# Softmax over 16384 rows: first loads issued from two queues, and a short store of zeros dropped

## The chip, the cores and the metric

The kernel runs on one core of a Trainium2 chip. The metric is device time in microseconds (us), from the start to the end of one execution; the median of several executions is used. A profile of one execution gives the span between its first and last recorded instruction, and a trace of all instructions and DMA transfers in it.

## The reference

The input x has the shape (32, 512, 1024) in float32 and the temperature is 0.5. The last axis is softmaxed:

```
scaled = x / temperature
shifted = scaled - max(scaled, axis=-1)
exp_x = exp(shifted)
out = exp_x / sum(exp_x, axis=-1)
```

That is 16384 rows of 1024 numbers: 67.1 MB are read and 67.1 MB are written.

## The kernel before

The rows are cut into 16 tiles of 1024 rows. A tile holds 8 rows in each of the 128 partitions, that is 32 KB in a partition and 4 MB (4096 KB) in all. There are six buffers for tiles (`BUFS = 6`, pool `data`). A tile is read into its buffer by one DMA, worked on in place, and written from the same buffer by one DMA.

The work on a tile comes in two groups of four rows per partition. For each group there are four steps:

- `maximum` (L70, L73): VectorE (DVE) takes the maximum of four rows in one TENSOR_REDUCE and multiplies it by -1/temperature, which gives a bias.
- `exponential` (L79): ScalarE (ACT) computes exp(x / temperature + bias) for one row per partition at a time, four times, and sums each row on the way.
- `divide` (L91, L93): DVE takes the reciprocal of the sums and multiplies the four rows by it.
- `store` (L101): after the second group of a tile, ACT's queue issues the store of the whole tile. Then `load` is called for the tile six places further on; this load goes to the buffer just stored, and so waits until the store has landed.

The order is written out by hand in the last loop: maximum and exponential of group g stand before divide and store of group g-1, so DVE takes the maximum of group g while ACT may still be at group g-1, and divides group g-1 while ACT works on group g.

All loads (L61) are issued from SP's queue, in the order of the tiles; all stores are issued from ACT's. An instruction that issues a DMA stands in the order of its engine: it waits for its semaphores there, and what is behind it on that engine waits too. SP does nothing but issue loads.

Ahead of the loop stand three things. DVE fills a small tile, `zeros`, of 512 bytes per partition (L111). ACT's queue issues a store of it into the first 128 columns of one row per partition of the first output tile (L112); the proper store of that tile later overwrites it. Then the first six loads are called.

Of the kernel before, what the change touches and what calls it, by code (L numbers as in the profile page):

```python
# [1 line left out]

# [4 lines left out]

TILES = [[8]] * 16  # L10
BUFS = 6

GROUP = 4


@with_exitstack
def kernel(
    ctx: ExitStack,
    tc: tile.TileContext,
    x: bass.AP,  # L20
    temperature: bass.AP,
    out: bass.AP,
):
    nc = tc.nc
    f32 = mybir.dt.float32
    scale = 1.0 / float(temperature)
    extreme = mybir.AluOpType.max if scale > 0 else mybir.AluOpType.min

    P = 128
    xf = x.flatten_outer_dims()  # L30
    of = out.flatten_outer_dims()
    n, d = xf.shape
    assert sum(sum(ks) for ks in TILES) * P == n

    data = ctx.enter_context(tc.tile_pool(name="data", bufs=BUFS))
    stats = ctx.enter_context(tc.tile_pool(name="stats", bufs=4))


    groups, first, r = [], [], 0
    for i, ks in enumerate(TILES):  # L40
        first.append(r)
        r += sum(ks)
        a = 0
        for k in ks:
            for b in range(0, k, GROUP):
                m = min(GROUP, k - b)
                groups.append((i, a + b, m, (a, k) if b + m == k else None))
            a += k

    def dram(t, i):  # L50
        k = sum(TILES[i])
        block = t[P * first[i] : P * (first[i] + k), :]
        return block.rearrange("(p k) d -> p k d", p=P, k=k)

    tiles, small = [], []

    def load():
        i = len(tiles)
        if i < len(TILES):
            xt = data.tile([P, sum(TILES[i]), d], f32, name="xt")  # L60
            nc.sync.dma_start(out=xt, in_=dram(xf, i))  # L61
            tiles.append(xt)

    def maximum(g):
        i, a, k, _ = groups[g]
        top, bias, sums, recip = (
            stats.tile([P, k], f32, name=name) for name in ("top", "bias", "sums", "recip")
        )
        small.append((bias, sums, recip))
        nc.vector.tensor_reduce(  # L70
            out=top, in_=tiles[i][:, a : a + k, :], axis=mybir.AxisListType.X, op=extreme
        )
        nc.vector.tensor_scalar_mul(bias, in0=top, scalar1=-scale)  # L73

    def exponential(g):
        i, a, k, _ = groups[g]
        bias, sums, _ = small[g]
        for b in range(k):
            nc.scalar.activation(  # L79
                tiles[i][:, a + b, :],  # L80
                tiles[i][:, a + b, :],
                mybir.ActivationFunctionType.Exp,
                bias=bias[:, b : b + 1],
                scale=scale,
                accum_out=sums[:, b : b + 1],
            )

    def divide(g):
        i, a, k, _ = groups[g]
        _, sums, recip = small[g]  # L90
        nc.vector.reciprocal(recip, sums)  # L91
        for b in range(k):
            nc.vector.tensor_scalar_mul(  # L93
                tiles[i][:, a + b, :], in0=tiles[i][:, a + b, :], scalar1=recip[:, b : b + 1]
            )

    def store(g):
        i, _, _, part = groups[g]
        if part:
            a, k = part  # L100
            nc.scalar.dma_start(out=dram(of, i)[:, a : a + k, :], in_=tiles[i][:, a : a + k, :])  # L101
            if a + k == sum(TILES[i]):
                load()

    zeros = stats.tile([P, 128], f32, name="zeros", bufs=1)
    with tc.manual_schedule():


        nc.vector.memset(zeros, 0.0)  # L111
        nc.scalar.dma_start(out=dram(of, 0)[:, 0, :128], in_=zeros)  # L112
        for _ in range(BUFS):
            load()
        for g in range(len(groups) + 1):
            if g < len(groups):
                maximum(g)
                exponential(g)
            if g > 0:
                divide(g - 1)  # L120
                store(g - 1)


# [1 line left out]
_INS = ['x', 'temperature']  # L125
_OUTS = [((32, 512, 1024), 'float32')]

_NUMBERS = {'temperature': 0.5}


# [26 lines left out]
```

## Time and profile before

| | |
|---|---|
| median of 4 runs | 318.34 us (318.18 to 318.73) |
| time of the profiled execution | 318.18 us |
| its span | 316.4 us |
| DVE busy | 235.6 us (74%) |
| ACT busy | 149.6 us (47%) |
| HBM read and written | 67.11 MB and 67.17 MB, 424 GB/s over the span |
| DMA packets | 4756, of which 528 under 512 bytes and 656 under 2 KB |
| a load, median time from issue to landing | 49.4 us |
| a store, the same | 39.4 us |
| the store of zeros, the same | 14.6 us |

The profile names a group of instructions by its line in the code, its engine, and the tile that it writes and reads: `xt<-in_x_dram` is a load, `out_dram<-xt` a store. SPq and ACTq are the queues from which DMAs are issued. The busy share of an engine is an average over the whole span; in the row of 40 slices each digit is the busy share in one fortieth (7.9 us), in tenths, and 9 stands for 90% or more. The time from issue to landing of a DMA holds the time that it stood behind others in its queue.

### The profile page before, as it was taken

How to read it: one execution, taken by the hardware profiler on the slowest of the kernel's cores; microseconds unless marked ns; L12 is line 12 of the kernel's file. 1: busy time of each engine (PE TensorE's matmuls, PEld its weight loads, DVE VectorE, ACT ScalarE, POOL GpSimd, SP SyncE). 2: the span in 40 equal slices, each digit the busy share in tenths (PEclk: the TensorE clock that was granted, in tenths of full speed). 3: DMA queues.
4: the chain of work that ended last, by engine and by line, in shares of the span. 5: the costliest groups of instructions: out<-in, count | busy, mean ns of one | idle time of the engine just before them, and what ended most of it. 6: DMA issues, size and time to landing. Idle time of an engine off the chain costs nothing.

```text
span 316.4 us, 623 instructions
## 1 busy us (share of the span) xinstructions
DVE 235.6 (74%) x225; ACT 149.6 (47%) x257; POOL 0.2 (0%) x4
## 2 busy tenths in 40 slices
DVE  0399999999689494994949859497793976949720
ACT  0176666666526255361554606556164561645500
POOL 0000000000000000000000000000000000000000
DMA  8999999999999999999999999999999999999995
GB/s 333 404 464 414 377 460 406 460 429 427 443 418 456 406 456 410 452 410 460 406 456 427 435 432 431 447 414 452 414 452 407 456 406 460 410 456 423 439 431 244
DMA packets 4756, 134.32 MB, mean 425 GB/s; under 512 B 528, under 2 KB 656, under 8 KB 656
## 3 DMA queue, kind: packets, MB, share of 16 engines
q1 hardware_dynamic: 2304, 67.11, 49.6%
q10 hardware_dynamic: 2448, 67.18, 49.2%
q14 instruction: 4, 0.03, 0.0%
HBM read 67.11 MB, written 67.17 MB: 424 GB/s over the span
## 4 chain that ended last, share of the span: by engine, by line
DMA 61%; DVE 28%; ACT 4%; another core or an unknown queue 1%; issue 1%; DVEq 0%; SPq 0%
DMA xt<-in_x_dram 35%; DMA out_dram<-xt 25%; DVE top L70 18%; DVE xt L93 9%; ACT xt L79 4%; DVE bias L73 1%; DVE recip L91 0%; DVEq L152 0%; SPq L61 0%
## 5 line engine op out<-in xcount | busy, mean ns | idle before, releaser
L79 ACT ACTIVATE xt<-xt,bias 128x1024 f32<-128x1024 f32 x128 | 145.4, 1137 | 136.8 <-DVE recip L91 119.4
L70 DVE TENSOR_REDUCE top<-xt 128x4 f32<-128x4096 f32 x32 | 141.3, 4416 | 61.7 <-DMA xt<-in_x_dram 61.7
L93 DVE TENSOR_SCALAR xt<-xt,recip 128x1024 f32<-128x1024 f32 x128 | 87.7, 749 | 1.1
L79 ACT ACTIVATION_READ_ACCUMULATOR xt<-xt,bias 128x1 f32 x128 | 23.8, 186 | 0.0
L79 ACT ACT_TABLE_LOAD x1 | 1.3, 1283 | 13.2 <-DMA xt<-in_x_dram 13.2
L91 DVE RECIPROCAL recip<-sums 128x4 f32<-128x4 f32 x32 | 5.5, 171 | 2.1 <-ACT xt L79 2.1
L73 DVE TENSOR_SCALAR bias<-top 128x4 f32<-128x4 f32 x32 | 5.4, 170 | 1.1
L111 DVE MEMSET zeros<- 128x128 f32 x1 | 0.2, 165 | 0.8 <-PEq L138 0.8
L138 POOL MEMSET const-uint8-127<- 128x1 uint8 x1 | 0.1, 103 | 0.0
L138 POOL MEMSET const-bfloat16-1.0<- 128x1 bf16 x1 | 0.1, 102 | 0.0
L138 POOL MEMSET const-float32-0.0<- 128x1 f32 x1 | 0.1, 99 | 0.2 <-issue 0.2
L138 POOL MEMSET const-float32-1.0<- 128x1 f32 x1 | 0.1, 99 | 0.0
## 6 DMA issues: line engine op xcount, KB each, us to landing
xt<-in_x_dram SPq DMA_DIRECT2D x16, 4096.0 KB, 49.4
out_dram<-xt ACTq DMA_DIRECT2D x16, 4096.0 KB, 39.4
out_dram<-zeros ACTq DMA_DIRECT2D x1, 64.0 KB, 14.6
```

What stands on the lines that cost most here:

```text
L70: nc.vector.tensor_reduce(out=top, in_=tiles[i][:, a : a + k, :], axis=mybir.AxisListType.X, op=extreme)
L73: nc.vector.tensor_scalar_mul(bias, in0=top, scalar1=-scale)
L79: nc.scalar.activation(tiles[i][:, a + b, :], tiles[i][:, a + b, :], mybir.ActivationFunctionType.Exp, bias=bias[:, b : b + 1], scale=scal ...
L91: nc.vector.reciprocal(recip, sums)
L93: nc.vector.tensor_scalar_mul(tiles[i][:, a + b, :], in0=tiles[i][:, a + b, :], scalar1=recip[:, b : b + 1])
L111: nc.vector.memset(zeros, 0.0)
L138: nc = _bacc.Bacc("TRN2", target_bir_lowering=False, num_devices=1)
```

## The change

The second, fourth and sixth of the six loads that first fill the buffers are issued from ACT's queue; the first, third and fifth, and all later loads, are issued from SP's as before. The tile `zeros`, its memset and its store are gone.

```diff
         if i < len(TILES):
             xt = data.tile([P, sum(TILES[i]), d], f32, name="xt")
-            nc.sync.dma_start(out=xt, in_=dram(xf, i))
+
+            queue = nc.scalar if i < BUFS and i % 2 else nc.sync
+            queue.dma_start(out=xt, in_=dram(xf, i))
             tiles.append(xt)
...
-    zeros = stats.tile([P, 128], f32, name="zeros", bufs=1)
     with tc.manual_schedule():
-
-
-        nc.vector.memset(zeros, 0.0)
-        nc.scalar.dma_start(out=dram(of, 0)[:, 0, :128], in_=zeros)
         for _ in range(BUFS):
             load()
```

On ACT the three loads now stand ahead of everything else: the load of the table for exp, the exponentials and the stores.

## The prediction
> **What bounds the kernel now.** I read the slices of the span first, then the table by stretches, then the waits, and last the chain.
>
> ```profile
> DVE  0399999999689494994949859497793976949720
> ACT  0176666666526255361554606556164561645500
> DMA  8999999999999999999999999999999999999995
> ```
>
> The DMA engines are full from the first slice to the last. DVE and ACT are full only until about 85 us; after that they wait. So the time is bytes over rate, plus whatever the DMA engines lose. The stretches below give that rate (the columns are the stretch, its length, busy DVE, ACT and POOL, clock, DMA share, GB/s).
>
> ```profile
> 5.00:31.00 26.00, 17.51 (x14) 11.46 (x18) 0.00 (x0) 1.00 1.01 435
> 31.00:41.00 10.00, 9.93 (x11) 7.25 (x15) 0.00 (x0) 1.00 0.99 393
> 41.00:90.00 49.00, 44.84 (x43) 28.84 (x50) 0.00 (x0) 1.00 1.00 432
> 90.00:280.00 190.00, 145.55 (x140) 92.58 (x160) 0.00 (x0) 1.00 1.00 433
> 283.00:312.00 29.00, 17.40 (x19) 9.28 (x16) 0.00 (x0) 1.00 1.00 432
> ```
>
> 5 to 31 us holds loads (and the small store of zeros); 41 to 280 loads and stores together; 283 to 312 stores alone. All run at 432 to 435 GB/s, so it makes no difference which kind is moved. The exception is 31 to 41 us, where the first large store (issued at 32.84) joins the running loads: 393 instead of 433 over 10 us, a loss of 10 x 40 / 433 = **0.92 us**. I call it the turn. The rest follows: 134.3 MB at 433 GB/s is 310.2 us, the turn 0.9, and 5.3 us of span are the start (first load issued at 0.73) and the thin end. The profiled execution took 318.18 us, 1.8 us more than its span of 316.4.
>
> ```profile
> DVE top L70 <- DMA xt<-in_x_dram: 61.7, 12, 12.2
> ...
> SPq L61 <- DMA out_dram<-xt: 215.8, 10, 44.6
> SPq L61 <- DMA xt<-in_x_dram: 9.9, 1, 9.9
> ```
>
> DVE waits 12 times for a load, SP's queue 10 times for a store that frees a buffer. SP waits once for a load: its sixth load was held until the first had landed at 13.1 us. None of these waits leaves the DMA engines idle, because another transfer is always queued. At the end:
>
> ```profile
> 232.93 49.80 DMA xt<-in_x_dram
> ...
> 282.75 4.43 DVE top L70
> ...
> 301.16 1.32 DVE xt L93 x2
> ```
>
> The last load lands at 282.7, and its store is issued at 302.5. The store before it, issued at 290.26, takes 15.4 us to land (305.7), so the DMA engines have work until 3.2 us after the last store is issued. The last store lands 12.8 us after its issue, at 315.3.
>
> **The change, part by part.**
>
> *Zeros removed.* One memset of 0.17 us on DVE, at 0.83, where DVE then waits 12.15 us for the first load: free. One issue of 0.41 us on ACT at 1.02, where ACT idles until 13.2: free. The first large store no longer follows it to the same output rows, but the zeros landed at 1.02 + 14.6 = 15.6, long before 32.84: free. What counts is 65.5 KB on the bound resource: 0.0655 MB / 433 GB/s = **-0.15 us**.
>
> *Three loads moved to ACT's queue.* By the order of instructions, ACT now issues three loads ahead of its table load and first exponential, and SP three, then ten. An issue took 0.36 to 0.56 us at this place on SP, so three are at most 1.7 us on ACT, under at least 12 us of idle time: free. The first packets can't come earlier, since SP's first load is first in its queue in both kernels.
>
> *The first tile lands later.* Loads 0 and 1 now run side by side. Before, load 0 landed at 13.1 and load 1 at 22.8 (issued at 1.1, 21.7 to landing). Shared evenly, both land at about 22: the bounds are 13.1, if SP's is served first, and 22.8. I take 22, nearest to even sharing. That two queues share evenly I take from the same table of issues: a load spaced 9.7 us from the next alone, a store every 19.35 us (134.49 to 153.84) when a load runs beside it. DVE starts 9 us later, and store 0 is issued at 22 + 19.7 = 42 instead of 32.84 (the first tile took 13.14 to 32.84). The cover is that the DMA engines keep loading: the loads come in pairs at 22, 42 and 61. DVE needs 14.8 us a tile (stores at 32.84, 47.61, 62.39), 237 us in all, and from 22 it could end at 264 with the last store's lag: well before the end.
>
> *Stores wait behind loads.* Stores 0 (42) and 1 (57) are queued behind load 5 on ACT's queue and start at about 61, alone, because all six buffers are full and SP has nothing to issue. Store 0 lands at about 71; then SP issues load 6. At 61 there is work for 2 x 9.7 us, to 80 us; store 2 comes at 72 and load 6 at 71, so the engines don't run dry. Without that cover, each us of idle time would cost a us. Load 6 lands at 91 to 95, before DVE asks for it at 22 + 6 x 14.8 = 111. From then on loads and stores alternate as before. ACT itself waits only for DVE at each store, as now.
>
> *The end.* Loads have the engines to themselves until 61 instead of about 35 (half of 26 us gained for loads, 13), then none of them from 61 to about 73 (half of 12 lost, 6). That lead of 7 us at full rate is 14 us when sharing: the last load lands at about 269 instead of 282.7, its store is issued at 289, and 4.5 stores are left then, to about 313. The margin of 3.2 us at the end grows to over 10. It buys nothing, since the engines were not idle there.
>
> *The turn.* This is the one price the trace doesn't show for the new order. Stores now follow loads on the same queue (61), and loads join running stores (71 to 75); besides, both queues start together. Bounds: the turn goes away (-0.92 us), or is paid once more (+0.92 us). I take one turn, no change: one stream still joins another running one, as at 32.84.
>
> Here a rule of the Trainium skill, "DMA: Bandwidth & Descriptors", section "Issuing engines are not separate DMA queues", speaks against any gain: DMAs from several engines run on the same 16 DMA engines and interleave, so that a second issuer saves issue time only. By that rule the turn has no price at all, in either kernel, and the sum is the zeros alone; the 393 GB/s above say that a joining queue isn't quite free.
>
> *Sum.* 318.18 - 0.15 + 0 = 318.03 us for the profiled execution. It is the fastest of the four runs, 0.16 below their median of 318.34. Compared median with median: 318.34 - 0.15 = **318.2 us**.
>
> **The rivals.** About 0.2% (0.64 us) is what a measurement of this kernel can tell from no change; so faster is below 317.70 and slower above 318.98.
>
> 1. *The turn goes away.* Store 0 stands right behind load 5 on one queue, so no new stream breaks in on a running one with a cold start, and load 6 joins only a short stretch of stores. For it: 90 to 280 us, where both queues always have work, shows no loss. Against: load 6 still joins. 318.2 - 0.92 = **317.3 us, faster**.
> 2. *The turn is paid twice*, once at the start, where ACT's loads join SP's, or at 61 when the stores begin, and once at 71 when load 6 comes back. For it: the only time in this trace that a large transfer joined from an empty queue, it cost 0.92 us. Against: the zeros joined the loads, and 5 to 31 us still ran at 435 GB/s (but they are only 64 KB). 318.2 + 0.92 = **319.1 us, slower**. It decides if the second turn costs over 0.8 us.
> 3. *The change doesn't do what it says:* ACT's first load starts so late that SP's first is served alone and lands near 13 us. Then compute starts as before, yet the sum is the same, **318.2 us**, for the engines are full either way.
>
> **How the numbers follow.** Forecast and third rival, within 0.2%: 0.51. First rival: 0.27. Second rival: 0.20, and 0.02 for a hole in the DMA work that I don't see (slower). So faster 0.27, same 0.51, slower 0.22. The likeliest case alone spans 317.7 to 318.9. The range reaches to both rivals, with a few tenths for where a turn falls on the slowest of the 16 engines: 317.0 to 319.3.
>
> **What would show it.** Right: DVE starts near 22 us; three loads from ACT; SP issues its fourth load near 71; the DMA row stays at 9 throughout; the last load lands near 269 and over 10 us of stores are queued when the last is issued; 432 to 435 GB/s in steady stretches; one dip of about 0.9 us between 60 and 85. No dip is rival 1; two dips, or one in the first 20 us too, rival 2; DVE starting near 13 is rival 3. The prediction is wrong in kind if a slice after 60 us shows idle DMA engines, or if loads in pairs run below 430 GB/s.

## The result, and the profile after

The changed kernel takes 317.92 us (median of 39 runs, 317.51 to 318.20); the kernel before takes 318.32 us (59 runs, 318.10 to 318.79). The ratio is 0.9986, with an interval of 0.9981 to 0.9990: 0.45 us less, or 0.14% (the two medians lie 0.40 us apart). The profiled execution took 317.88 us, its span was 316.1 us.

The slices of the span of the changed kernel, on its page:

```profile
DVE  0019999999999999999993976949669496794000
ACT  0015666666666655555565460645506455163000
DMA  8999999999999999999999999999999999999996
```

DVE starts one slice later, is then busy without a break until about 170 us instead of 85, and is done two slices earlier. The DMA engines are full from first to last, as before. The stretches of the changed kernel (stretch, length, busy DVE, ACT and POOL, clock, DMA share, GB/s):

```profile
5.00:31.00 26.00, 8.50 (x3) 5.16 (x8) 0.00 (x0) 1.00 1.00 430
31.00:41.00 10.00, 9.68 (x13) 6.97 (x13) 0.00 (x0) 1.00 0.98 423
50.00:70.00 20.00, 19.79 (x19) 11.70 (x22) 0.00 (x0) 1.00 0.97 396
90.00:280.00 190.00, 159.98 (x155) 102.01 (x176) 0.00 (x0) 1.00 1.00 433
283.00:312.00 29.00, 5.41 (x9) 4.37 (x8) 0.00 (x0) 1.00 1.00 433
```

The dip is gone from 31 to 41 us and stands between 50 and 70: the turn went with the first store. The waits of DVE and of SP's queue (total us, times, longest), and the chain that ended last (start, us, what):

```profile
DVE top L72 <- DMA xt<-in_x_dram: 51.0, 8, 22.5
...
SPq L63 <- DMA out_dram<-xt: 238.5, 10, 69.9
```

```profile
0.73 21.71 DMA xt<-in_x_dram
...
244.03 26.58 DMA xt<-in_x_dram
270.61 0.02 issue
270.63 4.43 DVE top L72
...
289.04 1.32 DVE xt L95 x2
```

DVE waits 8 times instead of 12, once for 22.5 us at the start. SP waits as often, at first for 69.9 us. The first tile is in at 22.4 us instead of 13.1, the last at 270.6 instead of 282.7. The last store is issued at 290.4 and takes 24.9 us to land, so that it lands at 315.3, just when the last store of the kernel before landed (302.51 + 12.8).

The stretches are a coarse measure of a dip: a packet is 32 KB and takes an engine 1.2 us, and an edge of a stretch cuts 16 of them. So I summed the bytes packet by packet from the trace, a packet cut by the edge counted in proportion, and took from each time what these bytes need at 433.3 GB/s, the rate of the steady stretches. What is left is the time that the DMA engines have lost by then, as a mean of the 16 (us; for the other columns see the experiments). By it the 423 GB/s from 31 to 41 us above are an effect of the edges: nothing was lost there.

```
by     before  after  no zeros  big zeros  first tile  last tile
 us                   (e1)      (e9)       halves(e10) halves (e11)
  5     2.59   2.47    2.65      2.68       2.54        2.64
 31     2.63   2.47    2.65      3.22       2.54        2.64
 41     3.43   2.46    3.25      3.22       2.53        3.53
 58     3.43   2.51    3.25      3.22       2.58        3.53
 66     3.49   3.59    3.31      3.22       3.67        3.59
280     3.66   3.82    3.52      3.51       3.93        3.98
300     3.67   3.85    3.53      3.52       3.97        3.99
308     3.68   3.85    3.74      4.37       3.97        4.01
```

Before, the turn cost 0.80 us between 31 and 41 us; after, 1.08 us between 58 and 66. One profile is one execution, and the size scatters: in the eight profiles of this case with the turn at 31 to 41 us it was 0.60 to 0.89 us (0.73 in the mean), in the four with six buffers and the split loads 0.87 to 1.09 (0.98 in the mean).

The engines don't stand idle in the turn. Before, 24 packets of the running loads, begun between 34.0 and 35.8 us, took 1.29 to 2.86 us where the others take 1.21; that makes 0.78 us per engine. The store's first packet runs at 37.2, behind them. After, it is 32 packets of the last loads, begun between 57.9 and 59.9 us, with 1.04 us per engine, and the store's first packet runs at 61.4.

All in all the engines lost 0.17 us more after (3.85 against 3.68) and had 0.15 us of zeros less to move. The two profiled executions thus reach their last landing within 0.1 us of each other, and yet their spans differ by 0.3 us. The rest lies behind the last landing. These are the DRAIN instructions of ACT and DVE that close the program (least, median and longest ns, first and last start in us), before and after:

```profile
L152 DVEq DRAIN  x2: 19/1396/2774, 299.8 to 315.8; - x2
L152 ACTq DRAIN  x2: 135/144/152, 302.9 to 316.0; - x2
```

```profile
L149 ACTq DRAIN  x1: 8/8/8, 315.7 to 315.7; - x1
L149 DVEq DRAIN  x1: 19/19/19, 315.7 to 315.7; - x1
```

Before, ACT's last DRAIN starts at 316.0, 0.2 us after DVE's, and takes 135 ns; after, it starts with DVE's and takes 8 ns. From the last landing to the end of the span there are 1.05 us before and 0.81 after.

### The profile page after: what moved, and what is told of

The parts are those of the page before. It is cut to its first block, busy times and chain, and to the rows that moved or that the text cites. A ratio compares the mean times of both kernels' runs of the same rounds, so it can differ in the third digit from the quotient of the medians.

```text
span 316.1 us, 619 instructions
## 1 busy us (share of the span) xinstructions
DVE 235.1 (74%) x224; ACT 149.6 (47%) x257; POOL 0.2 (0%) x4
## 4 chain that ended last, share of the span: by engine, by line
DMA 54%; DVE 32%; ACT 5%; issue 1%; DVEq 0%; SPq 0%
DMA xt<-in_x_dram 41%; DVE top L72 21%; DMA out_dram<-xt 13%; DVE xt L95 10%; ACT xt L81 5%; DVE bias L75 1%; DVE recip L93 1%; DVEq L149 0%; SPq L63 0%
## 5 line engine op out<-in xcount | busy, mean ns | idle before, releaser
L81 ACT ACT_TABLE_LOAD x1 | 1.3, 1283 | 22.5 <-DMA xt<-in_x_dram 22.5
```

Of the source, the lines that this page charges most:

```text
L81: nc.scalar.activation(tiles[i][:, a + b, :], tiles[i][:, a + b, :], mybir.ActivationFunctionType.Exp, bias=bias[:, b : b + 1], scale=scal ...
```

## The experiments

The questions were: which half of the change gains the 0.45 us; to what the turn belongs; what the end of the program has to do with it; and whether the late first tile is free by itself or by its cover. Ratios are to the kernel before, run beside it on the same chip.

### Each half alone

```diff
 e1: without zeros, all loads from SP's queue
-        nc.vector.memset(zeros, 0.0)
-        nc.scalar.dma_start(out=dram(of, 0)[:, 0, :128], in_=zeros)
```

> One half of the change alone: the store of zeros and its memset are gone, all loads stay on SP's queue. Theory 1 (the store costs its bytes, 0.0655 MB at 433 GB/s): 0.15 us less than before, a ratio of 0.9995. Theory 2 (its 128 small packets cost more than their bytes, and are all that the change gains): 0.4 us less, 0.9986, the whole of what the change gave. Theory 3 (the split of the loads gives the rest): as theory 1 here, and the rest in the kernel that only splits. In the stretches the turn, 0.92 us where the first large store joins, stays between 31 and 41 us by all of them.

Measured: 317.97 us, ratio 0.9987 (0.9979 to 0.9996). The gain is 0.4 us by the ratio, with 0.13 to 0.67 as its bounds: nearer to theory 2, but the 0.15 us of theory 1 is inside. The turn stayed between 31 and 41 us (0.60 us in the table).

```diff
 e2: split of the loads, zeros kept
-            nc.sync.dma_start(out=xt, in_=dram(xf, i))
+            queue = nc.scalar if i < BUFS and i % 2 else nc.sync
+            queue.dma_start(out=xt, in_=dram(xf, i))
```

> The other half alone: six loads from two queues, with the store of zeros kept ahead of ACT's loads. Theories 1 and 2: no change (ratio 1.000), since the DMA engines are full either way; the first TENSOR_REDUCE near 22 us and the turn near 60. Theory 3 (the split gains something at the start or the end): 0.2 to 0.3 us less, 0.9990 to 0.9994. If the turn is paid twice with two queues at the start: 0.9 us more, 1.003.

Measured: 318.00 us, ratio 0.9989 (0.9980 to 0.9998). So the split by itself gains something too, or something that came with it does; that it costs a second turn is excluded. Each half alone gives nearly the whole. Added up the halves would give 0.0024, the whole gave 0.0014; but each ratio here is known to about 0.0009 (0.3 us) only, so whether they add up isn't told.

```diff
 e3: zeros eight times as wide, as many packets
-    zeros = stats.tile([P, 128], f32, name="zeros", bufs=1)
+    zeros = stats.tile([P, 1024], f32, name="zeros", bufs=1)
-        nc.scalar.dma_start(out=dram(of, 0)[:, 0, :128], in_=zeros)
+        nc.scalar.dma_start(out=dram(of, 0)[:, 0, :], in_=zeros)
```

> The kernel before with zeros of 1024 columns in place of 128: the same 128 packets, 4096 bytes each instead of 512, 0.524 MB instead of 0.0655. By bytes it adds 0.459 MB / 433 GB/s = 1.06 us: ratio 1.0033 by theories 1 and 2, for the number of packets stays. If small packets cost their number and not their bytes: 1.000. If the turn is paid by the first real store, whatever its size, part of the 0.92 us moves from 31-41 us to where the zeros are stored, and the ratio stays near 1.0033; if the 4096-byte packets bring a turn of their own besides, 1.006.

Measured: 319.47 us, ratio 1.0028 (1.0018 to 1.0039), 0.6 to 1.2 us more. The price by bytes, 1.06 us, holds. That packets cost only their number is excluded, and so is a turn of their own for half a megabyte of zeros. The turn stayed between 31 and 41 us (0.63 us, summed as in the table).

### To what the turn belongs

```diff
 e4: the stores of tiles 6 and 7 held back until that of tile 8
+            held.append((i, part))
+            if i in (6, 7):
+                return
+            for j, (a, k) in held:
+                nc.scalar.dma_start(out=dram(of, j)[:, a : a + k, :], in_=tiles[j][:, a : a + k, :])
```

> The kernel before with the stores of tiles 6 and 7 held back until that of tile 8, so that ACT's queue runs empty near 153 us, loads alone run until near 166, and stores then join running loads a second time. The work of the DMA engines is the same and they should not idle. If each joining of stores to loads alone costs a turn (my theory after the result: the price belongs to stores that follow loads alone, not to a queue that comes alive): 0.92 us more, ratio 1.0029, and a second dip of about 0.9 us near 166 us. If the turn belongs to the first store of a program: 1.000 and no dip there. A row of idle DMA engines would spoil the reading.

Measured: 319.43 us, ratio 1.0041 (1.0020 to 1.0061), with runs from 318.50 to 321.72. The ratio fits neither expectation; the profile is clearer than the time. Three stretches of it: loads alone, stores joining them, and loads coming back:

```profile
150.00:166.00 16.00, 15.86 (x15) 9.27 (x16) 0.00 (x0) 1.00 1.01 434
166.00:178.00 12.00, 11.86 (x15) 8.82 (x15) 0.00 (x0) 1.00 1.00 431
```

```profile
190.00:206.00 16.00, 15.86 (x17) 10.50 (x19) 0.00 (x0) 1.00 0.98 397
```

Where stores join loads that run alone, at 166 us, nothing is lost: the theory that each joining costs a turn falls. Something is lost later, at 190 to 206 us, when SP's queue had run empty and loads came back: 0.90 us, again in slow packets and as much as a turn. The kernel before moved 432 GB/s there. Loads also came back from an empty queue in the changed kernel, at 72 us, and there nothing was lost but 0.07 us, all of it before the load's first packet at 75.9. Two 8 KB packets of the queue that the profile calls `instruction` run there, at 73.6 and 73.7 us. So coming back isn't by itself the price, and what it was in e4 stays open. The profiled run of e4 was its slowest, 321.72 us. Its last landing came 3.5 us later than in the kernel before: 1.0 us had been lost more by 310 us, and 2.6 us behind that, where the last packets of the engines end between 314 and 318.6 us instead of 313.2 to 315.0. The time goes by the engine that ends last. Why they end so far apart, and why these runs differ by 3 us among each other, stays open.

```diff
 e9: zeros of three whole rows per partition
-    zeros = stats.tile([P, 128], f32, name="zeros", bufs=1)
+    zeros = stats.tile([P, 3, 1024], f32, name="zeros", bufs=1)
-        nc.scalar.dma_start(out=dram(of, 0)[:, 0, :128], in_=zeros)
+        nc.scalar.dma_start(out=dram(of, 0)[:, 0:3, :], in_=zeros)
```

> The kernel before with zeros of 3072 columns, three whole rows per partition (1.57 MB in place of 0.0655), in the same place: where does the turn belong? By bytes 1.51 MB / 433 GB/s = 3.5 us more, ratio 1.0109. Theory 1 (the first large store of a program pays the turn): 0.6 to 1.1 us are lost between 5 and 20 us, and the stretch around 34 us, where the store of the first tile joins, runs at 433 GB/s. Theory 2 (the store of the first tile pays it, whatever came before): the stretch around 34 us is short by 0.6 to 1.1 us as before, and the start is not. Both: 1.013.

Measured: 321.92 us, ratio 1.0110 (1.0092 to 1.0128), as the bytes say. In its stretches:

```profile
5.00:31.00 26.00, 14.85 (x10) 10.45 (x17) 0.00 (x0) 1.00 1.01 426
28.00:48.00 20.00, 19.79 (x19) 11.42 (x21) 0.00 (x0) 1.00 1.00 434
```

The same stretch from 28 to 48 us of the kernel before:

```profile
28.00:48.00 20.00, 19.79 (x22) 12.46 (x21) 0.00 (x0) 1.00 0.99 411
```

The turn has moved to the start: 0.54 us are lost between 5 and 31 us (table), and nothing where the first tile's store joins. That is a little less than the 0.6 to 1.1 us of theory 1, and it comes in two steps, near 8 and near 14 us; but theory 2, a turn at the first tile's store whatever came before, is excluded. So an earlier large store takes the turn over. A store of 64 KB or 512 KB is not large enough for it (the turn stayed in its place with both), one of 1.5 MB is. This is one profile; e8, below, adds a condition. Their pieces differ too (512 bytes, 4 KB, 12 KB per partition), so whether the whole or the piece must be large isn't told apart.

```diff
 e10: the changed kernel, first tile stored in two halves
-TILES = [[8]] * 16
+TILES = [[4, 4]] + [[8]] * 15
```

> The changed kernel with its first tile stored in two halves, 16 KB per partition each, the first issued near 34 us instead of 42. If the turn is the time to read the first packets of a store ahead and grows with their size: half of the 0.9 to 1.1 us near 60 us, and 0.5 us less in all, ratio to before 0.997. If it is a fixed price, or has another cause: as the changed kernel, 0.9986, with the turn in its old place, since the halves too stand behind the last load on ACT's queue.

Measured: 318.05 us, ratio 0.9987 (0.9978 to 0.9996), and the turn in its place with its size (1.09 us in the table, 1.08 for the changed kernel):

```profile
50.00:70.00 20.00, 19.79 (x19) 11.71 (x21) 0.00 (x0) 1.00 0.98 397
```

Half the packet doesn't halve the turn. That a fixed number of bytes is read ahead, in packets of whatever size, isn't excluded by this.

### The end of the program

```diff
 e5: the kernel before and one more small instruction on ACT (e6: the changed kernel and three)
+                    extra = stats.tile([P, 1], f32, name="extra")
+                    nc.scalar.activation(
+                        extra, small[0][0][:, 0:1], mybir.ActivationFunctionType.Exp, scale=0.0
+                    )
```

> The kernel before with one more instruction on ACT (an exp of one column into a tile that nobody reads), early, where ACT has time. Reason: in the profile before, the span ends 1.05 us after the last landing, because ACT's DRAIN starts 0.2 us after those of the other engines and takes 135 ns; in the profile after it starts with them, takes 8 ns, and the span ends 0.81 us after the last landing. Zeros kept, loads on one queue. Theory A (how many instructions ACT's program has decides how its end is fetched, and this 0.24 us is the part of the gain that the prediction lacks): the DRAIN is prompt, the span ends 0.8 us after the last landing, 0.24 us less, ratio 0.9992. Theory B (the late DRAIN comes from the zeros or the queues): it stays late, ratio 1.000.

Measured (e5): 318.23 us, ratio 0.9998 (0.9989 to 1.0007). The DRAIN is prompt, 8 ns, and the span ends 0.85 us after the last landing:

```profile
L158 ACTq DRAIN  x2: 8/80/153, 303.1 to 315.9; - x2
```

> The changed kernel with three more instructions on ACT. Theory A in the form that every fourth count is a bad one (before had one less than after; three more than after is four more than before): the late DRAIN of 0.24 us returns, ratio to before 0.9995 instead of 0.9986. Theory A with one bad count only, and theory B: the DRAIN stays prompt, 0.9986. The three instructions themselves cost about 0.2 us each on ACT, which waits for DVE in most groups: nothing.

Measured (e6): 317.89 us, ratio 0.9987 (0.9978 to 0.9996), with a prompt DRAIN, 8 ns. That every fourth count is a bad one falls.

e12 is e1 with two such instructions, so that the trace has as many of ACT's instructions as in the kernel before.

> No zeros, all loads on SP's queue, and two more small instructions on ACT, so that its program has as many instructions in the trace as the kernel before (321), the count at which ACT's last DRAIN came late in all three kernels that had it. Theory A (that count makes the DRAIN late, and 0.24 us of the gain is that it no longer is): late DRAIN, the span ends 1.05 us after the last landing, and 0.24 us more than the kernel without zeros: ratio to before 0.9995, against 0.9987. Rival (the DRAIN is late but costs the time nothing, or depends on something else): 0.9987.

Measured: 318.07 us, ratio 0.9992 (0.9983 to 1.0001). The DRAIN is late again, though there are no zeros, and 1.01 us lie between the last landing and the end of the span:

```profile
L155 ACTq DRAIN  x2: 137/145/153, 302.8 to 315.9; - x2
```

In the trace ACT's program has 321 entries in the kernel before and in e3, e4, e7, e9 and e12, and the DRAIN is late in all six; it has 319, 320 or 322 to 325 (waiting and issuing entries counted) in the eight others, and the DRAIN is prompt in all eight. So the late DRAIN goes by the length of ACT's program, whatever the zeros or the queues do. Its price in the time is another matter: two pairs give 0.0002 (before and e5) and 0.0005 (e12 and e1), 0.06 to 0.16 us, against 0.2 us in the profiles, and both are inside the intervals of their runs. The 0.9992 of e12 lies between the two forecasts and tells them apart no better. It is likely, not shown, that it is part of the gain.

```diff
 e11: without zeros, all loads from SP's queue, last tile stored in two halves
-TILES = [[8]] * 16
+TILES = [[8]] * 15 + [[4, 4]]
```

> No zeros, all loads on SP's queue, and the last tile stored in two halves, so that a store is issued near 295 us that was issued near 302 before. Theory (the split of the loads gains its part by a margin at the end: in the unsplit kernels without zeros the engines ran at 406 GB/s from 300 to 308 us, since the last store came a little late): the hole at 300 to 308 us is closed and the time is that of the changed kernel, ratio 0.9985. Rival (the margin at the end gives nothing): as without zeros alone, 0.9987 to 0.9990.

Measured: 318.25 us, ratio 0.9996 (0.9987 to 1.0005). The small loss at the end (0.21 us from 300 to 308 us in e1) is closed to 0.02, but the time isn't better than without zeros alone; in the profiled executions the turn was 0.89 us instead of 0.60, which took it back there. The margin at the end gives no gain that can be measured here.

### The cover of the late first tile

```diff
 e7: four buffers, no zeros, all loads from SP's queue (e8: the changed kernel with four)
-BUFS = 6
+BUFS = 4
```

> Four buffers instead of six, no zeros, all loads on SP's queue: the pair of the next run. A tile's buffer is held for a load (9.7 to 19.4 us), 19.7 us of computing and a store (9.7 to 19.4 us) plus about 3 us, 62 us at most, and four buffers give 4 x 19.4 = 77 us: the DMA engines should still be nearly full. Ratio 1.000 to 1.005.

> Four buffers, no zeros, loads 0 and 2 on SP's queue, 1 and 3 on ACT's. My theory (the late first tile is free only because the six loads keep the engines busy until the first stores are there): the loads are done at 42 us, when the first store is issued; it is done at 52, load 4 is issued then and the second store at 57, so that the engines have a hole of 1 to 3 us there and thin spots until about 80: 1 to 6 us slower than four buffers on one queue. Rival (the order of the first loads never matters): the same as four buffers on one queue within 0.3 us.

Measured: e7 324.10 us, ratio 1.0192 (1.0164 to 1.0220), slower than expected; e8 328.41 us, ratio 1.0319 (1.0304 to 1.0335). The split costs 4.3 us with four buffers. The stretches around the first stores and at the end, e7 first:

```profile
40.00:50.00 10.00, 9.93 (x9) 6.47 (x12) 0.00 (x0) 1.00 0.98 423
50.00:60.00 10.00, 9.86 (x11) 5.23 (x9) 0.00 (x0) 1.00 0.97 419
...
280.00:300.00 20.00, 15.36 (x15) 9.92 (x18) 0.00 (x0) 1.00 0.75 323
```

```profile
40.00:50.00 10.00, 9.93 (x12) 7.25 (x13) 0.00 (x0) 1.00 0.80 344
50.00:60.00 10.00, 9.93 (x8) 6.02 (x12) 0.00 (x0) 1.00 0.81 315
...
280.00:300.00 20.00, 15.38 (x16) 9.93 (x19) 0.00 (x0) 1.00 0.88 382
```

In e8 the four loads are in at 42 us, when the first store is only issued, and the engines stand idle for about a us from 42 and again from 53 us, before and behind that store: (433 - 344) x 10 / 433 + (433 - 315) x 10 / 433 = 4.8 us; summed by packets, 4.4 us by 58 us, more than the hole of 1 to 3 us that I expected. My theory holds: with six buffers two more loads are still to run when the first store comes, and they are what makes the late first tile free. Most of what e7 adds to the kernel before lies at its end, where 323 GB/s for 20 us are 5.1 us lost: with four buffers the last stores are used up before the last tile is computed. I had left the end out of that expectation.

e8 also says more of the turn. Its first store, a whole tile, finds idle engines; it runs alone from 43.1 us and lands at 53.3. These are its stretches with the first store alone, and around the second store:

```profile
46.00:52.00 6.00, 5.93 (x8) 4.64 (x8) 0.00 (x0) 1.00 1.02 437
56.00:70.00 14.00, 13.86 (x14) 8.50 (x15) 0.00 (x0) 1.00 1.00 412
```

By packets, 0.02 us are lost in the first. In the second 0.70 us are lost between 58 and 63 us, with busy engines, in slow packets of the running load; the first packet of the second store runs at 61.9, behind them. So it isn't the first large store that pays, but the first that joins running loads. This fits all 14 profiles. That it is paid only once is no rule: slow packets of the same kind cost 0.90 us in e4 (190 to 206 us) and about 0.4 in e7 (64 to 68 us) and in e6 (220 to 225 us), at places for which I have no rule.

## Why the prediction was right, and where it was not

The result, 0.9986, lies in the class that I gave the most chance (within 0.2%) and inside the range. The value, 318.2 us, was 0.3 us too high: I forecast 0.14 us of gain, and there were 0.40 between the medians.

**What bounds the kernel:** right. Nine tenths or more in every slice of the DMA row but the first and the last in both kernels, 430 to 435 GB/s wherever nothing turns, whether loads, stores or both run. The first wait of DVE that grew to 22.5 us, 61.7 us of waits that shrank to 51.0 and a last tile that came 12 us earlier moved the last landing by less than 0.1 us.

**The first tile:** right. DVE starts at 22.5 us (22 was taken) and store 0 is issued at 42.2 (42). Loads 0 and 1, issued together at 0.73, took 21.7 and 21.9 us to land, side by side. The Trainium skill, "DMA: Bandwidth & Descriptors", section "Queues, rings and completion order", says that each DMA engine takes turns between queues, packet by packet; the two landings 0.2 us apart agree.

**Stores behind loads, and the cover:** right. SP's fourth load was issued at 72.1 (71), landed at 95.5 (91 to 95: half a us late), and no slice ran dry. With four buffers the cover is gone and 4.3 us appear.

**The end:** the steps were right (last load in at 270.6, predicted 269; last store issued at 290.4, predicted 289). The store before the last landed at 305.6, so the margin grew from 3.2 to 15.2 us ("over 10"). The "4.5 stores" of the prediction are those left when the last load lands, at 269; when the last store is issued about 2.5 are left (24.9 us). That the larger margin buys nothing is what e11 leaves standing, though the margin of 3.2 us before was thinner than it looked: without zeros 0.21 us were lost at the end, with big zeros 0.85 by 308 us.

**The turn:** right in its count (one), half right in its mechanism, and its size shifted. I took it for the price of a stream that joins a running one, and expected it between 60 and 85 us, perhaps with load 6. The change has two such joinings, and I had no reason to charge one of them and not the other: that one was right is in part luck. It came between 58 and 62 us, with the first store, and load 6 joined for nothing. e9 and e8 show what it goes with: the first large store that joins running loads. e4 shows that a later joining of stores is free. Neither rival's mechanism was seen: with loads on two queues at the start nothing was paid twice, and nothing went away, for the first store still joined running loads. The 0.92 us of the prediction came from a stretch with cut edges; by packets it was 0.80 before, and 1.08 after.

**The sum, the step that was mis-sized:** "65.5 KB on the bound resource ... -0.15 us". The 0.45 us of the ratio have room for three things. By pairs of kernels that differ in one of them: without zeros 0.0008 (before and e12), 0.0011 (e5 and e1) and 0.0003 (e2 and after), in the mean 0.0007 or 0.23 us; prompt DRAIN 0.0002 and 0.0005, in the mean 0.11 us; split 0.0009 (e5 and e2) and 0.0001 (e1 and after), in the mean 0.16 us. They add up to 0.50 us, near enough to 0.45. But no pair is outside its error, about 0.0009 for a ratio and more for a difference of two, so that the division stays open. The profiles even speak against the split in one place, for its turn is 0.25 us larger in the mean; about 0.1 us of a gain shows at the start, where the four profiles with the split and without zeros had lost 2.47 to 2.54 us by 5 us and the ten others 2.59 to 2.70. What else the split gains isn't known. Firm is this much: the whole is 0.32 to 0.60 us, the zeros' bytes alone are too little for it, and the end of the program, a term that I had put at nothing without looking, holds 0.24 us of the 0.3 by which the two profiled spans differ. For the zeros there is a reason to cost more than their bytes: in the trace each engine carries eight of their packets at 27 ns each, 0.22 us in all, where 512 bytes at the full rate would take 19 ns.

## What to carry to other kernels

When one resource is full from the first slice to the last, find what a change adds to or takes from that resource and from the two ends; how tiles arrive, which engine waits and how long only matter once the cover runs out, and that is a matter of counting how many transfers are queued when the next one can first be issued (six buffers: free; four: 4.3 us). A dip in the rate that stands beside an event isn't yet the price of that event: make the event happen twice, earlier, or alone, before calling it a rule. For changes of a tenth of a per cent, compare the stretch from the last landing to the end of the span as well, and expect that parts cannot be told from each other.

## What the runs showed of the hardware that I had not expected

- The first large store that joins running loads slows these loads for a moment: 0.54 to 1.09 us were lost, whether its first packet ran at 7.7 us (e9), 37 us or 61 us, in 12 KB, 16 KB or 32 KB pieces. 64 KB and 512 KB of zeros ahead of it didn't take it over, and a first store that ran alone (e8) paid nothing. The cause isn't known from these runs, and slow packets of the same kind came later too in three of the 14 profiles.
- A queue that comes alive beside a busy one gets its first packet late: store 0 was issued at 32.84 us in the kernel before, and its first packet ran at 37.2; load 6 of the changed kernel was issued at 72.1, its first packet ran at 75.9. In e8, on idle engines, store 0 was issued at 42.2 and its first packet ran at 43.1.
- ACT's closing DRAIN came 0.2 us late at one length of ACT's program, 321 entries in the trace, in six of six kernels, and in none of eight with other lengths.
